# A two-block transformer forward pass: the last product before each run of up products cut in two, and the first norm's factors spread into PSUM by two products

## The chip, the cores and the metric

The kernel runs on one core of a Trainium2 chip, in one launch. The metric is the time of one execution on the device in microseconds (us), lower is better. Before the change the median of three runs is 964.23 us (964.13 to 964.59). Five engines matter here: TensorE (PE) multiplies, its weight loads shown apart as PEld; VectorE (DVE), ScalarE (ACT) and GpSimd (POOL) do everything element by element; SyncE (SP) issues the transfers (DMA).

## The reference, cut to what matters

256 tokens of width 1024 go through two transformer blocks with different mixers, all in float32.

```python
h = rms_norm(x, mix_pre_norm)                       # the first norm: x * rsqrt(mean(x^2) + eps) * factors
mix = hybrid_token_mixer(h, w_in, ...)              # attention, block attention, gated delta rule
x = x + rms_norm(mix, mix_post_norm)
u = causal_depthwise_conv(rms_norm(x, ffn_pre_norm) @ w_up, conv_w) + conv_b
gate, up = split(u)
x = x + rms_norm((gelu(gate) * up) @ w_down, ffn_post_norm)     # 22 blocks up, 11 down
# second model, two layers on the same x
x = x + gmlp_mixer(rmsnorm(x), a_w_in, ..., a_w_out)            # 8 blocks up, 8 down
x = x + square(relu(rmsnorm(x) @ w1_0)) @ w2_0                  # 16 up, 16 down
x = x + mla_mixer(rmsnorm(x), latent_kv(x), ...)
x = x + square(relu(rmsnorm(x) @ w1_1)) @ w2_1                  # 16 up, 16 down
out = rmsnorm(x, final_norm_g)
```

## The kernel before, in words

Tokens lie in two tiles of 128. To keep float32 accuracy every operand of a large product is split into a high and a low part (`split`: ACT copies the high part, DVE subtracts it for the low part), and every product becomes three (`mm3`: high by high, high by low, low by high). In the profile a weight chunk is `raw` when it lands, then `s0h`, `s0l` to `s7h`, `s7l`; normalised tokens are `xTh`, `xTl`; activations between an up and a down product are `aT0h`, `aT0l` and so on.

A large product stands in one of two forms. In `fm` the loaded operand is 128 columns of weights and the streamed one is the 256 tokens (`r_fm<-xTh,s2h 128x256`). In `tm` the loaded operand is one tile of 128 tokens and the weights are streamed: 392 columns in the first projection `w_v`, 256 in the first blocks of a stage, 512 in the down products (`r_acc<-s0h,r_aT0h 128x512`). The names after the arrow are the streamed operand, then the loaded one.

`updown` runs the four feed-forward stages: after a lag of four blocks it alternates `down` (24 products of 512 columns into the four banks `acc0`, `acc1`) with `up` (48 products of 256 columns into `r_fm`; two such ups between two downs in the first feed-forward layer). The last four downs of a stage run together at its end, tile 0 first, and tile 1's part is finished by `last_downs`.

The order of all instructions is made when the kernel is built. Python generators (threads) yield one operation at a time, and `run_threads` always emits the one that an estimate of costs (`Estimate.cost`) says can start first; ranks of 10 and more wait a little. Each engine then works through its own list strictly in that order. So a change of a cost, of a rank or of one operation near the start changes what is chosen for a long way behind it.

Weights come in halves of 128 x 1024 into a ring of four `raw` buffers (`RAW`); `dma_next` issues the next one after a half has been split (`split_piece`). At the start `main` issues, on SP's queue, the two halves of token tile 0, the identity `c_ident`, the 1024 factors of the first norm repeated on 128 partitions (`gb`, 512 KB written), one half of `w_v`, token tile 1, and three more halves. `warm_up` lets PE multiply zeros while nothing else is there, until the estimate says 8 us. `junction` does the first norm of each tile: ACT sums the squares of both halves, DVE and POOL make the root (`rstd`), DVE multiplies x by it and by `gb` (`r_xg`), PE transposes into `r_tp`, ACT and DVE split that into `xTh`, `xTl`.

Of the kernel before, what the change touches and what calls it, by code (L numbers as in the profile page):

```python
# [13 lines left out]
AF = mybir.ActivationFunctionType  # L14
ALU = mybir.AluOpType
AX = mybir.AxisListType

P = 128
D = 1024
EPS = 1e-6  # L20
LAG = 4
TAIL = 4
STAG, STAGF, STAGV = 3, 4, 4
SLOTS, EXTRA, PREF = 4, 1, 10.0
RAW = 4
AHEAD, CLOSE, URGENT = 5, 1, 3
DEFER = 0.3
SLACK = 0.02
WARM = 8.0
BIG = 1e30  # L30
LINE = 128
HALF = LINE // 8
# [1 line left out]
HALVES = (slice(0, 512), slice(512, 1024))  # L34
# [41 lines left out]
class Estimate:  # L76
# [14 lines left out]
    def cost(self, eng, op, aps, args, t):  # L91
        n = max(a.free_size() for a in aps)
        psum = any(a.space == bass.MemoryType.PSUM for a in aps)
        if eng == "PE":
            n = aps[2].free_size() * (4 if aps[1].dtype == F32 else 1) if op == "matmul" else 2 * P
            tick = int(t / self.TICK)
            slow = self.columns.get(tick - 1, 0.0) < 3060.0
            self.columns[tick] = self.columns.get(tick, 0.0) + n * aps[1].partition_size() / P
            return n / 1200.0 if slow else n / 2400.0 + 0.0023
        if eng == "ACT":  # L100
            t = self.TABLES.get(args[2], self.table)
            load, self.table = (1.28 if t != self.table else 0.0), t
            return load + (0.05 if psum else 0.09) + n / 1200.0 + 0.09 * (len(aps) - 2)
        if eng == "DVE":
            if op == "reciprocal":
                return 0.07 + n / 120.0
            fast = not psum and len(aps) == 2 and op in ("tensor_scalar", "tensor_copy")
            return (0.13 if op == "scalar_tensor_tensor" else 0.07) + n / (1920.0 if fast else 960.0)
        return 0.5 if op == "memset" else 0.3 + n / 6.0

    def start(self, use):

# [85 lines left out]
class Kernel:  # L198
# [138 lines left out]

    def can_split(self):
        c = self.chunks.get(self.split_at)
        if c is None or c.pieces == len(c.raw):  # L340
            return False
        return bool(c.pieces or self.free_slots())

# [109 lines left out]
            yield from self.T.transpose(dst[:, b * P:(b + 1) * P], src[:, b * P:(b + 1) * P], self.ident)  # L453


    def mm3(self, o, lh, ll, rh, rl, first, last):
        T = self.T
        yield from T.matmul(o, lh, rh, start=first, stop=False)
        yield from T.matmul(o, lh, rl, start=False, stop=False)
        yield from T.matmul(o, ll, rh, start=False, stop=last)  # L460

    def fm(self, o, w, c0, xT, nk):

# [2 lines left out]
            yield from self.mm3(o, w[0][:, k, c0:c0 + P], w[1][:, k, c0:c0 + P], xT[0][:, k, :], xT[1][:, k, :],  # L466
                     k == 0, k == nk - 1)

    def tm(self, o, w, xT, t, ks, k0=0, c0=0, n=None, first=True, last=True, ev=None):

        n = n or w[0].shape[2]
        ts = slice(t * P, (t + 1) * P)
        for i, k in enumerate(ks):
            yield from self.block_ready(w, k)
            if ev and (k0 + k) % 4 == 0:
                yield self.on((ev, t, (k0 + k) // 4))
            yield from self.mm3(o, xT[0][:, k0 + k, ts], xT[1][:, k0 + k, ts], w[0][:, k, c0:c0 + n], w[1][:, k, c0:c0 + n],
                     first and i == 0, last and i == len(ks) - 1)

    def new_acc(self, t):  # L480
        acc = []
# [1 line left out]
            acc.append((yield from self.bank("acc%d" % t)))  # L483
        return acc

    def down(self, acc, w, aT, t, k0, first, last):
        last = last if isinstance(last, tuple) else (last, last)
        for h in range(2):
            yield from self.tm(acc[h], w, aT, t, (0, 1), k0=k0, c0=h * 512, n=512, first=first, last=last[h])
            if last[h]:  # L490
                self.set(("sum", acc[h].name, 512 * h), acc[h])

# [35 lines left out]
    def junction(self, t, dests, acc=None, post=None):  # L528
# [4 lines left out]
        for g, xT, ev in dests:  # L533
# [15 lines left out]
                self.set((ev, t, h), xT[1])  # L549
            self.set((ev, t), xT[1])  # L550


    def updown(self, names, n, per, pool, block, aT, tail, stagger, gains=(), final=False):

# [26 lines left out]
        for kind, i in updown_plan(n, per):  # L581
# [10 lines left out]
            if acc is None:  # L592
                acc = [[], []]
# [3 lines left out]
            yield self.on((names[0], "block", i))  # L597
            if i < nd - TAIL:
                yield from self.down(acc[0], c.view(2), aT[i], 0, 0, i == 0, False)
                yield from self.down(acc[1], c.view(2), aT[i], 1, 0, i == 0, (False, final and i == nd - TAIL - 1))  # L600
                self.free(c)
                self.rel(aT[i][0])
            else:
                yield from self.down(acc[0], c.view(2), aT[i], 0, 0, i == 0, i == nd - 1)
                last.append((i, c))
# [22 lines left out]
            if cols.stop == D:  # L628
                self.free(c)

    def warm_up(self):

        z = self.tile(self.pers, [P, D], "zero", tag="gb", bufs=2)[:, :P]
        yield from self.G.memset(z, 0.0)
        z = z.bitcast(BF16)
        o = yield from self.bank("acc1")
        while self.est.free["PE"] < WARM:
            yield from self.T.matmul(o[:, :256], z[:, :P], z, start=True, stop=True)
        self.rel(o)
# [28 lines left out]
    def main(self, ctx):  # L668
# [10 lines left out]

        load_x(0)  # L680
        self.ident = self.load(self.consts, "ident")
        g = self.gain("mix_pre_norm")
        self.dma_next()
        load_x(1)
        for _ in range(RAW - 1):
            self.dma_next()
        self.junk_tile = self.tile(self.scr, [P, 512], "junk")
        self.tile(self.scr, [P, 2], "mv", bufs=2)
# [2 lines left out]
        self.one = self.tile(self.consts, [P, 1], "one")  # L691
        yield from self.G.memset(self.one, 1.0)
        self.pad(self.consts, 2 * HALF)
        self.spawn(20, self.warm_up())
        self.hT = self.new_xT()
        for t in range(2):
            self.spawn(0, self.junction(t, [(g, self.hT, "w_in")]))
        with ExitStack() as s:
            yield from self.mixer(self.pool(s, "mix"))
        self.add_slots(self.pool(ctx, "second"), 1)  # L700
# [928 lines left out]
```

## Time and profile before

| | |
|---|---|
| runs | 964.13, 964.23, 964.59 us; median 964.23 |
| the profiled execution | 963.24 us, of which the span is 961.5 |
| PE busy | 939.2 us of the span, 6475 products |
| DVE, ACT, POOL busy | 648.4, 515.0, 24.9 us |
| transfers | 168.22 MB, 175 GB/s over the span |

The span runs from the first to the last instruction. All products and element operations carry one line number, since they are recorded by a helper (L177), so groups are told apart by tile names. PE's products overlap one another (the busy time of one is longer than its distance to the next), so what a stream of products costs is read from the starts, not from the durations.

### The profile page before, as it was taken

The numbers are of one execution on the slowest core, as the hardware profiler recorded it, in microseconds if no ns is written. First come the engines' busy times: TensorE is split into PE (matmuls) and PEld (weight loads), VectorE is DVE, ScalarE is ACT, GpSimd is POOL, SyncE is SP. The second block draws the span as 40 slices with busy tenths as digits, with TensorE's granted clock in tenths as the row PEclk, the third lists the DMA queues.
The fourth block names the chain that finished last, engine by engine and source line by source line (L and its number), as shares of the span: only waits on it lengthen the run. The fifth ranks groups of instructions, "written<-read, shape, count | busy, mean of one in ns | idle before, by whom it ended". The sixth has DMA issues, their size and how long they took to land.

```text
span 961.5 us, 16153 instructions
## 1 busy us (share of the span) xinstructions
PE 939.2 (98%) x6475; PEld 863.1 (90%) x6475; DVE 648.4 (67%) x1027; ACT 515.0 (54%) x853; POOL 24.9 (3%) x38
## 2 busy tenths in 40 slices
PE   7999999999999999999998999999999999999997
PEld 6899878899999989999988999998889899999986
DVE  5687776889687757697557765554678687555533
ACT  5664565767566546535445644444557575444421
POOL 0000000000000001000000000000110000000000
PEclk8999999999999999999999999999999999999999
DMA  7732432746777637727645776564345377566511
GB/s 230 252 111 89 132 110 88 223 132 197 254 227 233 201 113 287 244 88 259 193 133 152 244 226 192 192 194 148 96 149 161 111 231 240 186 202 194 193 47 44
DMA packets 48891, 168.22 MB, mean 175 GB/s; under 512 B 6448, under 2 KB 7088, under 8 KB 48560
## 3 DMA queue, kind: packets, MB, share of 16 engines
q1 hardware_dynamic: 48816, 167.19, 54.5%
q8 instruction: 51, 0.84, 0.4%
q14 instruction: 24, 0.20, 0.1%
HBM read 166.12 MB, written 1.05 MB: 174 GB/s over the span
## 4 chain that ended last, share of the span: by engine, by line
PE 90%; DVE 3%; ACT 2%; DMA 2%; issue 1%; SPq 1%; POOL 0%; POOLq 0%; DVEq 0%; ACTq 0%
PE r_fm L177 47%; PE r_acc L177 38%; PE r_tp L177 5%; DMA x<-x 1%; DMA vm<-inv_freq 1%; ACT junk L177 1%; DVE r_xg L177 1%; DVE cT L177 1%; DMA raw<-w_up 1%; DVE s4l L177 0%; POOL rstd L177 0%; DVE s3l L177 0%; DVE s0l L177 0%; DVE xTl L177 0%; ACT cT L177 0%
## 5 line engine op out<-in xcount | busy, mean ns | idle before, releaser
L177 DVE TENSOR_TENSOR s0l<-raw,s0h 128x1024 fp32r<-128x1024 f32 (+1 forms) x54 | 64.8, 1211 | 19.8 <-ACT s0h L177 19.7
L177 DVE TENSOR_TENSOR s2l<-raw,s2h 128x1024 fp32r<-128x1024 f32 (+1 forms) x54 | 65.1, 1212 | 17.4 <-ACT s2h L177 17.2
L177 DVE TENSOR_TENSOR s3l<-raw,s3h 128x1024 fp32r<-128x1024 f32 (+1 forms) x56 | 66.8, 1201 | 14.9 <-ACT s3h L177 14.7
L177 DVE TENSOR_TENSOR s1l<-raw,s1h 128x1024 fp32r<-128x1024 f32 (+2 forms) x54 | 64.8, 1201 | 15.5 <-ACT s1h L177 15.2
L177 ACT ACTIVATE s0h<-raw 128x1024 fp32r<-128x1024 f32 (+1 forms) x54 | 55.6, 1046 | 26.4 <-PE r_acc L177 17.2
L177 PE MATMUL r_fm<-xTh,s1h 128*128 128x256 f32 x240 | 67.3, 280 | 0.0
L177 PE MATMUL r_fm<-xTl,s1h 128*128 128x256 f32 x240 | 67.3, 280 | 0.0
L177 PE MATMUL r_fm<-xTh,s1l 128*128 128x256 f32 x240 | 67.3, 280 | 0.0
L177 DVE TENSOR_TENSOR s4l<-raw,s4h 128x1024 fp32r<-128x1024 f32 (+1 forms) x46 | 55.2, 1210 | 16.7 <-ACT s4h L177 16.7
L177 ACT ACTIVATE s3h<-raw 128x1024 fp32r<-128x1024 f32 (+1 forms) x56 | 57.5, 1036 | 16.8 <-PE r_acc L177 10.2
L177 ACT ACTIVATE s2h<-raw 128x1024 fp32r<-128x1024 f32 (+1 forms) x54 | 56.0, 1045 | 16.7 <-PE r_acc L177 9.7
L177 DVE TENSOR_TENSOR r_q<-r_r 128x512 f32<-128x512 f32 x32 | 22.1, 692 | 62.1 <-ACT r_r L177 62.0
L177 ACT ACTIVATE s1h<-raw 128x1024 fp32r<-128x1024 f32 (+2 forms) x54 | 55.9, 1037 | 14.4 <-DMA raw<-w_up 5.3
L177 ACT ACTIVATE r_r<-r_fm 128x512 f32<-128x512 f32 x26 | 15.6, 599 | 80.5 <-PE r_fm L177 80.5
L177 ACT ACTIVATE s4h<-raw 128x1024 fp32r<-128x1024 f32 (+1 forms) x46 | 47.4, 1043 | 18.8 <-PE r_acc L177 9.8
L177 PE MATMUL r_fm<-xTh,s3h 128*128 128x256 f32 x200 | 56.3, 281 | 0.4 <-DVE cT L177 0.4
L177 PE MATMUL r_fm<-xTl,s3h 128*128 128x256 f32 x200 | 56.2, 281 | 0.0
L177 PE MATMUL r_fm<-xTh,s3l 128*128 128x256 f32 x200 | 56.1, 281 | 0.0
L177 PE MATMUL r_fm<-xTl,s2h 128*128 128x256 f32 x176 | 49.4, 281 | 0.0
L177 PE MATMUL r_fm<-xTh,s2l 128*128 128x256 f32 x176 | 49.4, 280 | 0.0
L177 PE MATMUL r_fm<-xTh,s2h 128*128 128x256 f32 x176 | 49.3, 280 | 0.0
L177 POOL TENSOR_TENSOR rstd<-rstd,mhalf 128x1 f32<-128x1 f32 (+1 forms) x30 | 23.9, 798 | 931.4 <-DVE rstd L177 914.7
(611 smaller groups left out, 3153.8 us busy)
## 6 DMA issues: line engine op xcount, KB each, us to landing
raw<-w SPq DMA_DIRECT2D x128, 512.0 KB, 4.6
raw<-w_up SPq DMA_DIRECT2D x44, 512.0 KB, 4.8
raw<-w_down SPq DMA_DIRECT2D x22, 512.0 KB, 4.9
raw<-a_v SPq DMA_DIRECT2D x16, 512.0 KB, 5.6
raw<-a_u SPq DMA_DIRECT2D x16, 512.0 KB, 4.5
raw<-a_w_out SPq DMA_DIRECT2D x16, 512.0 KB, 4.7
raw<-w_c SPq DMA_DIRECT2D x12, 512.0 KB, 5.2
raw<-w_out SPq DMA_DIRECT2D x8, 512.0 KB, 3.7
```

The lines of the kernel that those rows point to most:

```text
L177: f(*args, **kw)
```

## The change

The last product of a down block into the second bank of tile 1, 128x512, is issued as two of 128x256 with the same loaded operand (`cut=256`), for all downs but the last four of each stage. The first norm no longer reads its factors from a tile of 128 rows: one row of 4 KB is loaded, and two products with a loaded row of ones (`gain_banks`) spread it into two PSUM banks, behind 16 products of zeros. The square of the second half moves from ACT to DVE. The first weight half may be chosen for splitting only once both normalised halves of tile 0 have been issued, and the next chunks only once tile 0 has been transposed and split. The estimate takes less for a `memset`, and the zeros run on until it says 10 us. Token tile 1 is loaded after two halves of `w_v`, not after one.

```diff
@@ -26,7 +26,7 @@
...
-WARM = 8.0
+COLD, WARM = 16, 10.0
...
@@ -106,7 +106,7 @@
...
-        return 0.5 if op == "memset" else 0.3 + n / 6.0
+        return 0.1 + n / 1280.0 if op == "memset" else 0.3 + n / 6.0
...
@@ -337,7 +337,7 @@
...
     def can_split(self):
         c = self.chunks.get(self.split_at)
-        if c is None or c.pieces == len(c.raw):
+        if c is None or c.pieces == len(c.raw) or ("xg" if self.split_at == 0 else ("w_in", 0)) not in self.ev:
             return False
         return bool(c.pieces or self.free_slots())
...
@@ -453,11 +453,13 @@
...
-    def mm3(self, o, lh, ll, rh, rl, first, last):
+    def mm3(self, o, lh, ll, rh, rl, first, last, cut=None):
         T = self.T
         yield from T.matmul(o, lh, rh, start=first, stop=False)
         yield from T.matmul(o, lh, rl, start=False, stop=False)
-        yield from T.matmul(o, ll, rh, start=False, stop=last)
+        parts = (slice(0, cut), slice(cut, None)) if cut else (slice(None),)
+        for c in parts:
+            yield from T.matmul(o[:, c], ll, rh[:, c], start=False, stop=last and c is parts[-1])
...
         ts = slice(t * P, (t + 1) * P)
...
             yield from self.mm3(o, xT[0][:, k0 + k, ts], xT[1][:, k0 + k, ts], w[0][:, k, c0:c0 + n], w[1][:, k, c0:c0 + n],
-                     first and i == 0, last and i == len(ks) - 1)
+                     first and i == 0, last and i == len(ks) - 1, cut if i == len(ks) - 1 else None)
...
@@ -483,10 +485,11 @@
...
-    def down(self, acc, w, aT, t, k0, first, last):
+    def down(self, acc, w, aT, t, k0, first, last, cut=None):
         last = last if isinstance(last, tuple) else (last, last)
         for h in range(2):
-            yield from self.tm(acc[h], w, aT, t, (0, 1), k0=k0, c0=h * 512, n=512, first=first, last=last[h])
+            yield from self.tm(acc[h], w, aT, t, (0, 1), k0=k0, c0=h * 512, n=512, first=first, last=last[h],
+                               cut=cut if h else None)
             if last[h]:
                 self.set(("sum", acc[h].name, 512 * h), acc[h])
...
@@ -548,6 +551,45 @@
...
+    def gain_banks(self, row):
+
+        banks = []
+        for h in HALVES:
+            o = yield from self.bank("acc0", row)
+            yield from self.T.matmul(o, self.one[:1, :].to_broadcast([1, P]), row[:, h], start=True, stop=True)
+            banks.append(o)
+        self.first_gain = banks
+        self.set("first gain", *banks)
+
+    def first_norm(self, t):
+
+        S, V, x = self.S, self.V, self.x[t]
+        ss = self.sums()
+        if t:
+            yield self.on(("w_in", 0, 0))
+        yield from S.activation(self.junk(512), x[:, HALVES[0]], AF.Square, accum_out=ss[:, 0:1])
+        xg = []
+        for h in range(2):
+            xg.append((yield from self.take(self.scr, [P, 512], "xg")))
+        yield from V.scalar_tensor_tensor(xg[1], x[:, HALVES[1]], 1.0, x[:, HALVES[1]], op0=ALU.mult, op1=ALU.mult,
+                                          accum_out=ss[:, 1:2])
+        r = yield from self.rstd(ss, 1, D, 2)
+        yield self.on("first gain")
+        for h in range(2):
+            yield from V.scalar_tensor_tensor(xg[h], x[:, HALVES[h]], r, self.first_gain[h], op0=ALU.mult, op1=ALU.mult)
+        self.set("xg")
+        if t:
+            self.rel(*self.first_gain)
+        for h in range(2):
+            tp = yield from self.bank("tp", xg[h])
+            yield from self.transposes(tp, xg[h], 4)
+            self.rel(xg[h])
+            sl = (slice(None), slice(4 * h, 4 * h + 4), slice(t * P, (t + 1) * P))
+            yield from self.split(self.hT[0][sl], self.hT[1][sl], tp.rearrange("p (k c) -> p k c", k=4))
+            self.rel(tp)
+            self.set(("w_in", t, h), self.hT[1])
+        self.set(("w_in", t), self.hT[1])
...
@@ -597,7 +639,8 @@
...
             if i < nd - TAIL:
                 yield from self.down(acc[0], c.view(2), aT[i], 0, 0, i == 0, False)
-                yield from self.down(acc[1], c.view(2), aT[i], 1, 0, i == 0, (False, final and i == nd - TAIL - 1))
+                yield from self.down(acc[1], c.view(2), aT[i], 1, 0, i == 0, (False, final and i == nd - TAIL - 1),
+                                     cut=256)
                 self.free(c)
...
@@ -628,12 +671,15 @@
...
-    def warm_up(self):
+    def warm_up(self, row):
 
         z = self.tile(self.pers, [P, D], "zero", tag="gb", bufs=2)[:, :P]
         yield from self.G.memset(z, 0.0)
         z = z.bitcast(BF16)
         o = yield from self.bank("acc1")
+        for _ in range(COLD):
+            yield from self.T.matmul(o[:, :256], z[:, :P], z, start=True, stop=True)
+        self.spawn(0, self.gain_banks(row))
         while self.est.free["PE"] < WARM:
             yield from self.T.matmul(o[:, :256], z[:, :P], z, start=True, stop=True)
         self.rel(o)
@@ -679,10 +725,13 @@
 
         load_x(0)
         self.ident = self.load(self.consts, "ident")
-        g = self.gain("mix_pre_norm")
-        self.dma_next()
+        row = self.tile(self.pers, [P, D], "row", tag="gb", bufs=2)[:1, :]
+        self.nc.sync.dma_start(row, ap["mix_pre_norm"][None, :])
+        self.est.dma(row, 4 * D)
+        for _ in range(2):
+            self.dma_next()
         load_x(1)
-        for _ in range(RAW - 1):
+        for _ in range(RAW - 2):
             self.dma_next()
...
-        self.spawn(20, self.warm_up())
+        self.spawn(20, self.warm_up(row))
         self.hT = self.new_xT()
         for t in range(2):
-            self.spawn(0, self.junction(t, [(g, self.hT, "w_in")]))
+            self.spawn(0, self.first_norm(t))
```

PE, at the start of the program (rows 37 to 42 of the changed kernel; `zero` is the tile of zeros, `row` the row of factors, `one` a column of ones). The zeros ahead and behind are the same pair of rows again.

```order
L177 LDWEIGHTS zero
L177 MATMUL r_acc_111<-zero 128x256
L177 MATMUL r_acc_134<-row,one 128x512
L177 MATMUL r_acc_136<-row,one 128x512
L177 LDWEIGHTS zero
```

There are 19 products of zeros ahead of the two new ones; behind them stand 11, then four transposes of `r_xg`, 5 zeros, four transposes, 10 zeros and the first product of `w_v`. Before, 26 zeros, four transposes, 3 zeros and four transposes stood ahead of it.

DVE, at the start of the program, before (`x_74` and `x_75` are the two token tiles).

```order
L177 TENSOR_TENSOR rstd<-ss 128x1
L177 TENSOR_SCALAR rstd<-rstd 128x1
L177 SCALAR_TENSOR_TENSOR r_xg<-x_74,rstd,gb 128x512 x2
L177 TENSOR_TENSOR s0l<-raw,s0h 128x784
L177 TENSOR_TENSOR xTl<-r_tp,xTh 128x4x128
L177 TENSOR_TENSOR rstd<-ss 128x1
L177 TENSOR_SCALAR rstd<-rstd 128x1
L177 TENSOR_TENSOR xTl<-r_tp,xTh 128x4x128
L177 SCALAR_TENSOR_TENSOR r_xg<-x_75,rstd,gb 128x512 x2
L177 TENSOR_TENSOR s0l<-raw,s0h 128x784
```

The same place of DVE's list in the changed kernel.

```order
L177 SCALAR_TENSOR_TENSOR r_xg,ss<-x_74 128x512
L177 TENSOR_TENSOR rstd<-ss 128x1
L177 TENSOR_SCALAR rstd<-rstd 128x1
L177 SCALAR_TENSOR_TENSOR r_xg<-x_74,rstd,r_acc_134 128x512
L177 SCALAR_TENSOR_TENSOR r_xg<-x_74,rstd,r_acc_136 128x512
L177 TENSOR_TENSOR s0l<-raw,s0h 128x784
L177 TENSOR_TENSOR xTl<-r_tp,xTh 128x4x128
L177 TENSOR_TENSOR s0l<-raw,s0h 128x784
L177 TENSOR_TENSOR xTl<-r_tp,xTh 128x4x128
L177 SCALAR_TENSOR_TENSOR r_xg,ss<-x_75 128x512
L177 TENSOR_TENSOR s1l<-raw,s1h 128x784
```

Both halves of the first weight chunk now stand ahead of everything of token tile 1, whose norm has moved behind them.

PE, at the product that waits for the gates of the delta rule (`gates`, made by ACT and DVE from the columns of `w_v`), with the difference to before.

```order
 L177 MATMUL r_fm<-xTh,s3l 128x256
 L177 MATMUL r_fm<-xTh,s3h 128x256
+L177 MATMUL r_fm<-xTl,s3h 128x256
+L177 MATMUL r_fm<-xTh,s3l 128x256
+L177 MATMUL r_fm<-xTh,s3h 128x256
+L177 MATMUL r_fm<-xTl,s3h 128x256
+L177 MATMUL r_fm<-xTh,s3l 128x256
+L177 MATMUL r_fm<-xTh,s3h 128x256
 L177 MATMUL r_tp<-gates,c_mix_consts 128x8
 L177 MATMUL r_tp<-gates,one 128x8
```

Six products of the projection that runs there have moved ahead of it. Behind this place PE's list differs for some 517 products of the mixer (different ones chosen first, the same ones in all); from the end of its attention on, it is the same as before but for the cuts.

PE, at the end of the first down block of the first feed-forward layer, in the changed kernel (`r_acc_2684` is the second bank of tile 1).

```order
L177 MATMUL r_acc_2684<-s0h,aT0l 128x512
L177 MATMUL r_acc_2684<-s0h,r_aT0h 128x512
L177 MATMUL r_acc_2684<-s0l,r_aT0h 128x512
L177 MATMUL r_acc_2684<-s0h,aT0l 128x256 x2
L177 MATMUL r_fm<-xTh,s1h 128x256
L177 MATMUL r_fm<-xTl,s1h 128x256
```

Before, the row with x2 was one product `128x512`. There are 35 such places; behind 31 of them stands a run of up products (six runs of 96, three of 48, twice eleven of 48), behind the other four the last downs of the stage.

## Rows read from the trace of the kernel before

**Rows 1.** The page, part 1: engine, busy us, share, instructions.

```profile
PE 939.2 (98%) x6475; PEld 863.1 (90%) x6475; DVE 648.4 (67%) x1027; ACT 515.0 (54%) x853; POOL 24.9 (3%) x38
```

**Rows 2.** Busy time by stretch (window, length, each engine's busy us, granted clock, DMA).

```profile
12.00:20.00 8.00, 6.96 (x32) 5.53 (x32) 7.39 (x12) 5.56 (x9) 0.56 (x1) 0.81 0.53 158
...
42.00:152.00 110.00, 108.60 (x848) 97.30 (x847) 89.23 (x211) 66.97 (x168) 5.58 (x6) 1.00 0.37 118
...
515.00:690.00 175.00, 175.00 (x1128) 159.91 (x1128) 104.18 (x131) 85.93 (x116) 0.55 (x1) 1.00 0.58 182
```

**Rows 3.** The chain that ended last, up and down blocks (start us, us, what).

```profile
232.58 5.46 PE r_acc L177 x24
238.03 11.31 PE r_fm L177 x96
...
544.08 5.65 PE r_fm L177 x48
```

**Rows 4.** The same view, runs of 256 columns elsewhere.

```profile
200.95 30.16 PE r_fm L177 x266
...
379.88 24.15 PE r_fm L177 x205
...
407.91 10.20 PE r_fm L177 x90
...
525.14 1.77 PE r_fm L177 x15
...
527.26 1.94 PE r_fm L177 x17
```

**Rows 5.** Timeline of PE (start us, us, engine, line, op, out<-streamed,loaded).

```profile
198.49 0.28 PE L177 MATMUL r_fm<-s4h,xTl 128*128 128x256 f32 x1
...
198.94 0.28 PE L177 MATMUL r_fm<-xTh,s0h 128*128 128x256 f32 x1
...
199.42 0.28 PE L177 MATMUL r_fm<-xTl,s0h 128*128 128x256 f32 x1
```

**Rows 6.** Timeline of the start, all engines (in brackets idle time before, and its releaser).

```profile
1.06 4.78 PE L177 MATMUL r_acc<-zero 128*128 128x256 bf16 x26 [1.06 <-POOL zero L177]
...
2.11 0.43 SPq L294 DMA_DIRECT2D gb<-mix_pre_norm  x1
...
5.68 0.55 POOL L177 TENSOR_TENSOR rstd<-rstd,mhalf 128x1 f32<-128x1 f32 x1 [4.68 <-DVE rstd L177]
8.77 1.41 DVE L177 SCALAR_TENSOR_TENSOR r_xg<-x,rstd,gb 128x512 f32<-128x512 f32 x2 [3.24 <-DMA gb<-mix_pre_norm]
...
9.84 0.86 ACT L177 ACTIVATE s0h<-raw 128x784 fp32r<-128x784 f32 x1 [4.69 <-DMA raw<-w_v]
...
11.84 0.68 PE L177 MATMUL r_fm<-s0h,xTh 128*128 128x392 f32 x1
...
21.11 1.23 DVE L177 TENSOR_TENSOR s2l<-raw,s2h 128x1024 fp32r<-128x1024 f32 x1 [0.80 <-ACT s2h L177]
```

**Rows 7.** DMA issues of the first 30 us (KB each, median us to landing).

```profile
c_ident<-ident SPq DMA_DIRECT2D x1, 64.0 KB, 4.3
```

**Rows 8.** All products of zeros (ns min/median/max, first and last start).

```profile
L177 PE MATMUL r_acc<-zero x29: 272/421/421, 1.1 to 10.9; 128*128 128x256 bf16 x29
```

**Rows 9.** Busy time in two stretches of 1 us, as in rows 2.

```profile
7.00:8.00 1.00, 0.00 (x0) 0.00 (x0) 0.00 (x0) 0.00 (x0) 0.00 (x0) 1.00 1.00 387
8.00:9.00 1.00, 0.00 (x0) 0.00 (x0) 0.23 (x1) 0.00 (x0) 0.00 (x0) 0.57 1.06 408
```

**Rows 10.** Timeline around the first projections and the gates.

```profile
24.50 0.28 PE L177 MATMUL r_fm<-xTh,s2h 128*128 128x256 f32 x1
...
31.29 1.06 ACT L177 ACTIVATE s1h<-raw 128x1024 fp32r<-128x1024 f32 x1 [1.76 <-DMA raw<-w_c]
...
36.67 0.36 PE L177 MATMUL r_tp<-gates,c_mix_consts 128*128 128x8 f32 x2 [2.35 <-issue]
...
40.52 1.72 PE L177 MATMUL r_acc<-c_mix_consts,gates 128*128 128x128 f32 x14
```

More of the change, by code (lines that the diff above doesn't have):

```diff
@@ L467, in fm, with tm @@
                      k == 0, k == nk - 1)
-    def tm(self, o, w, xT, t, ks, k0=0, c0=0, n=None, first=True, last=True, ev=None):
+    def tm(self, o, w, xT, t, ks, k0=0, c0=0, n=None, first=True, last=True, ev=None, cut=None):
         n = n or w[0].shape[2]
```

## The prediction

> **What bounds the kernel now.** I read the page's first part, the busy times by stretch, the chain of waits through the feed-forward stages, and the timeline of the first 40 us. PE is busy for 939.2 of 961.5 us [rows 1]; through the stages of up and down blocks it never pauses (175.00 of 175 us) while DVE has 104 and ACT 86 us of work there [rows 2]. So two things can move the end: what one product costs in those stages, and what PE waits for at the start.
>
> The reader is to see in the chain of waits what a product costs. Down: 24 in 5.46 us, 0.2275 each. Up: 96 in 11.31, 0.1178 each; 48 in 5.65, the same [rows 3]. But there are runs of the same shape at another distance: 266 in 30.16 is 0.1134, 90 in 10.20 is 0.1133, 205 in 24.15 is 0.1178 [rows 4]. So 256 columns have two levels, 0.1134 and 0.1178, and a run keeps its level for hundreds of products. All the runs of up products that follow a down block lie at the higher one.
>
> Where does the level change? In the pieces 379.88 and 407.91 PE does not pause between the two: the stage goes over from the token-major form to the feature-major one (the streamed and the loaded operand change places) and falls from 0.1178 to 0.1133. Pieces 525.14 (15 in 1.77, 0.118) and 527.26 (17 in 1.94, 0.114) lie on either side of the same exchange [rows 4]. At 198.94 the exchange finds a run at the lower level, four in 0.45 us, and leaves it at the higher, four in 0.48 [rows 5]. So in these three cases an exchange between products of 256 columns turns the level over. After a down block the exchange comes too, but with it the change from 512 to 256, and the run is at the higher level.
>
> At the start PE waits for the first norm. Its factor is there at 5.68 + 0.55 = 6.2 us, but DVE begins the normalised halves at 8.77, having waited for the factors that are repeated on 128 rows; the first product of `w_v` starts at 11.84 [rows 6]. From then on DVE is full (7.39 of 8 us) [rows 2] until it has the second remainder of the next weight chunk at 21.11 + 1.23 = 22.3 [rows 6], and PE starts that projection at 24.50 [rows 10].
>
> **The cut.** It divides 35 products. Two of 256 columns at the higher level are 0.2356 against 0.2275: 35 x 0.008 = 0.3 us lost. Behind 31 of them stands a run of ups, 6 x 96 + 3 x 48 + 22 x 48 = 1776 products. Now the last thing ahead of the exchange is two products of 256 columns in the token-major form, which is the situation of [rows 4], no longer 512 columns. If the exchange turns the level over as it did there, the runs fall to 0.1134: 1776 x 0.0044 = 7.8 us won, all of it on the path, since PE is the only full engine there. The first products behind an exchange may still stand at the higher spacing; for three of them at each of 31 entries I take off 0.4. Sum: -7.8 + 0.3 + 0.4 = -7.1. The ends are +0.3 (no run changes) and -7.8 (every one, the cut itself free). I take the end with the turn, because the three exchanges between equal sizes are the nearest rows to the new order; the runs after 512 columns are the nearest to the old one.
>
> The Trainium skill (TensorE: Matmul & The Clock Gate, Back-to-back issue gap) gives one gap for one size, columns by the full clock plus about 2.5 ns, and nothing on what stood ahead. By that rule the cut would cost 35 x 2.5 ns = 0.09 us as an estimate, and win nothing, which is rival 1 below. The trace has two levels for one size [rows 4], so it does not agree.
>
> **The start.** The row of 4 KB takes the broadcast's place in SP's queue, right behind the identity, which lands 4.3 us after its issue at about 1.64, so at 5.9 [rows 6, 7]. I take 5.9 for the row too. On PE it is queued behind 19 products of zeros. Zeros come at two speeds (421 and 272 ns) [rows 8]: 256 columns are 0.213 us at 1.2 GHz and 0.107 at 2.4, and 26 in 4.78 us fit 17 slow and 9 fast ones. So 19 end near 1.06 + 17 x 0.213 + 2 x 0.11 = 4.9, and PE waits about 1 us. A float32 product of 128 columns shows as two records: 14 records in 1.72 us are seven products, 0.21 to 0.25 each [rows 10], so one of 512 columns is about 0.86 at full clock. The factors are in PSUM at 6.8 and 7.6, DVE's first normalised half starts at about 7.0 instead of 8.77. Behind them on PE stand 26 more zeros (2.8 us) and eight transposes (0.11 each, 0.9): the first product of `w_v` cannot start before 7.6 + 3.7 = 11.3, 0.5 earlier than before. The zeros hide nothing here; they stand ahead of the transposes.
>
> What counts is DVE's list, which is the bound until 22.3. It began at 8.77 and took 13.6 us; the changed list is the same plus one square of 128x512 (the other falls into the wait), priced by the normalising row, 1.41 / 2 = 0.7 [rows 6]. A factor read from PSUM instead of a tile of 128 rows has no row; I take the same duration, between none and 0.1 more for each of four. Starting at 7.0 it would end at 21.3; the waits for weights in the old list shrink, since the broadcast's 512 KB are gone from the queue and the first weight half no longer lands only at 9.84. Lower end 7.0 + 13.6 - 0.8 (the wait at 21.11) = 19.8, upper end 22.3. I take 20.8: -1.5 us at 24.50.
>
> Next is the product that waits for the gates: PE idles 2.35 us ahead of it, at 36.67, and the chain goes back to a weight half that landed at 31.29 [rows 10]. That half's buffer is freed by DVE's list, so it comes 1.5 earlier as well. In PE's new order six more products (6 x 0.113 = 0.7) stand ahead of it and fill part of the wait. Start and gates together: -2.2, ends 0 and -3.7 (the whole 2.35 filled with -1.4 ahead of it).
>
> **The mixer's order** is another one for 517 products. PE is idle for 1.4 of the 110 us there [rows 2], so at best 1.4 is won; as much may be lost. I take 0.
>
> **Sum.** -7.1 - 2.2 = -9.3. The profiled execution took 963.24, 0.99 below the median 964.23, so it would become 953.9, and the median 954.9.
>
> **Rivals.** (1) *The level stays.* A run after down products is at 0.1178 wherever one follows [rows 3], and two products between may be too few to change what 512 columns have set. Against it stand [rows 4, 5]. Then -2.2 + 0.3: 962.3.
> (2) *The start is given back.* Rival 1, and what is ahead at 24.50 is lost in the mixer's new order, where PE's strict list meets other waits: +0.3, at most a stall or two of about 1 us: 964.5. For it: the order is made by an estimate that left 2.35 us of waiting at the gates. Against: only 1.4 us of idle time there so far.
> (3) *The row comes late; slower.* PE's list is strict, so everything waits behind the two factor products. Before, PE stopped at 5.8, and the granted clock was 1.00 in the window from 7 us and 0.57 in that from 8 [rows 9]: it fell after 2 to 3 us of rest. If the row lands as late as the broadcast did, near 8.6, PE has rested 3.7 us and works at half clock: two factors 3.4 us, 26 zeros 5.5, transposes 1.7, so `w_v` starts at 19.2 instead of 11.84, and its 48 products of 392 columns (0.163 each at 2.4 GHz, 7.8 us) end at 27.0, 2.5 later than 24.50. With the runs at the old level: 964.2 + 0.3 + 2.5 = 967.0. It decides from a landing of about 7.5 on. Against it: 4 KB instead of 512.
>
> **Chances.** Forecast 0.65, by itself 952.7 (all ends good) to 957.5 (a part of the runs turns). Rival 1 0.18, rival 2 0.10, rival 3 0.07. About 0.2% (1.93 us: below 962.3 and above 966.2) is what a measurement tells from no change. Faster: 0.65 and half of rival 1, 0.74. Same: the other half and rival 2, 0.19. Slower: 0.07. The range reaches over rival 1 into rival 2, 952.0 to 964.5, and leaves out the others with half of rival 2, and a little below.
>
> **What would show it.** In the chain of waits, pieces of 48 ups of 5.45 us instead of 5.65 and of 96 of 10.9 instead of 11.31, beside down pieces of 5.46; the first product of `w_v` near 11.3, the projection at 24.50 near 23.0, the wait at the gates under 1.7. Wrong: up pieces still at 5.65 and the time at 962 (rival 1), that and an idle time in the mixer of 3 us (rival 2), or a granted clock of 0.5 while the zeros run behind the factors (rival 3).

## The result, and the profile after

The five executions of the changed kernel took 956.09, 956.88, 960.05, 961.25 and 3311.51 us, a median of 960.05 beside 964.13 of the kernel before (963.34 to 964.59). The last one was disturbed and does not count in the ratio: the other four have a median of 958.47, ratio 0.9942, 95% interval 0.9921 to 0.9962. In a second series (`after_again`, below) the changed kernel took 956.60 (954.39 to 961.16) beside 965.62: 0.9909 (0.9890 to 0.9928). It is faster in both; 954.9 was predicted. Its times spread over 5 us in the first series and 7 in the second, which the prediction did not expect; the experiments explain a part of that.

The profiled execution took 956.88 (before 963.24). Part 1 of its page answers [rows 1], the busy times by stretch answer [rows 2]; the columns are those named there.

```profile
PE 935.2 (98%) x6531; PEld 859.5 (90%) x6531; DVE 648.8 (68%) x1031; ACT 515.1 (54%) x849; POOL 26.4 (3%) x38
```

```profile
12.00:20.00 8.00, 6.53 (x38) 5.87 (x38) 7.52 (x14) 4.75 (x6) 1.23 (x1) 1.00 0.76 251
42.00:152.00 110.00, 107.64 (x832) 95.96 (x831) 86.86 (x201) 67.52 (x166) 7.39 (x6) 1.00 0.33 106
515.00:690.00 175.00, 175.00 (x1151) 159.81 (x1150) 104.44 (x126) 88.88 (x123) 2.56 (x3) 1.00 0.58 184
```

In the last window PE still never pauses. Its 1151 products beside 1128 are no measure of the win, since 24 of them are halves of divided products and the window lies some 4 us further on in the program. PE's busy time fell by 4.0 us although 56 instructions came to it. The chain of waits of the changed kernel says where, and answers [rows 3]:

```profile
230.34 5.46 PE r_acc L177 x25
235.80 10.90 PE r_fm L177 x96
...
440.34 5.46 PE r_fm L177 x48
```

96 ups take 10.90 instead of 11.31, 48 take 5.46 instead of 5.65, and the down piece with its one product more still 5.46. All 31 runs behind a division show this. The start, in the timeline of all engines, answers [rows 6, 10]:

```profile
1.06 3.83 PE L177 MATMUL r_acc<-zero 128*128 128x256 bf16 x19 [1.06 <-POOL zero L177]
...
2.11 0.33 SPq L729 DMA_DIRECT2D row<-mix_pre_norm  x1
...
4.82 1.98 PE L177 MATMUL r_acc<-row,one 1*128 1x512 f32 x4
...
5.80 0.55 POOL L177 TENSOR_TENSOR rstd<-rstd,mhalf 128x1 f32<-128x1 f32 x1 [4.79 <-DVE rstd L177]
6.38 1.41 DVE L177 SCALAR_TENSOR_TENSOR r_xg<-x,rstd,r_acc 128x512 f32<-128x512 f32 x2 [0.74 <-POOL rstd L177]
...
10.37 0.42 PE L177 MATMUL r_fm<-s0h,xTh 128*128 128x392 f32 x1
```

The row is there by 4.82, and PE goes from the zeros to the factors almost without a stop (two starts 0.20 us apart), where before it stood idle for 3.73 us ahead of the first transposes. DVE now waits for POOL's factor (0.74), no longer for the load (3.24). The normalising of two halves reads PSUM at the old price, 1.41. Where the granted clock stood at 0.57 in the microsecond from 8 [rows 9], it is 1.00:

```profile
7.00:8.00 1.00, 1.00 (x12) 0.91 (x10) 0.79 (x2) 0.60 (x1) 0.00 (x0) 1.00 0.98 368
8.00:9.00 1.00, 1.00 (x11) 0.94 (x10) 0.71 (x1) 0.68 (x2) 0.00 (x0) 1.00 1.06 412
```

From the first starts of the same products in the timelines of PE, the program falls into eight stretches. Three of the experiments stand beside the two (us):

| stretch, up to | before | after | cut_only | start_only | early_again |
|---|---|---|---|---|---|
| first w_qk product | 24.50 | 21.97 | 24.92 | 21.95 | 22.47 |
| exchange at 199 (mixer, out, w_up) | 174.44 | 174.78 | 175.36 | 174.27 | 174.84 |
| token-major a_v at 361 | 162.12 | 159.77 | 161.03 | 162.06 | 161.04 |
| token-major w1 at 503 | 142.36 | 141.87 | 141.88 | 142.36 | 141.88 |
| exchange at 527 | 23.68 | 25.09 | 24.43 | 25.57 | 18.91 |
| token-major w1 at 775 | 247.74 | 246.03 | 246.03 | 247.87 | 245.97 |
| exchange at 794 | 18.82 | 19.64 | 19.12 | 20.28 | 18.94 |
| last product | 160.79 | 158.95 | 159.34 | 160.79 | 158.95 |

Between before and after: the start -2.53, the mixer +0.34, the four stretches with divisions -2.35 - 0.49 - 1.71 - 1.84 = -6.39, and two junctions, which nobody had touched, +1.41 and +0.82. Sum -6.35.

### The profile page after: what moved, and what is told of

Read it like the earlier page. It is cut to its first block, busy times and chain, and to the rows that moved or that the text cites. A ratio compares the mean times of both kernels' runs of the same rounds, so it can differ in the third digit from the quotient of the medians.

```text
span 955.1 us, 16271 instructions
## 1 busy us (share of the span) xinstructions
PE 935.2 (98%) x6531; PEld 859.5 (90%) x6531; DVE 648.8 (68%) x1031; ACT 515.1 (54%) x849; POOL 26.4 (3%) x38
## 4 chain that ended last, share of the span: by engine, by line
PE 88%; DVE 4%; DMA 2%; ACT 2%; issue 1%; POOL 1%; SPq 1%; POOLq 0%; DVEq 0%; ACTq 0%
PE r_fm L177 46%; PE r_acc L177 37%; PE r_tp L177 5%; DMA vm<-inv_freq 1%; POOL rstd L177 1%; ACT junk L177 1%; DVE r_xg L177 1%; DMA raw<-w_v 1%; DMA raw<-w 1%; DVE s1l L177 0%; DVE xTl L177 0%; DMA raw<-w_up 0%; DVE s4l L177 0%; DVE s0l L177 0%; DVE s3l L177 0%
```

## The experiments

**Each half of the change alone, the change again, and the division in another place.** The kernel before with the division only (`cut_only`), the changed kernel with `cut=None` (`start_only`), the changed kernel unedited (`after_again`), and the kernel before with the division in the first half of the block:

```diff
-                               cut=cut if h else None)
+                               cut=None if h else cut)
```

> The kernel before with the 35 divided products alone; start and mixer as before. Theory (two products of 256 columns ahead of the exchange turn the runs of up products to the lower level, 0.1134 to 0.1138 instead of 0.1178): 31 runs, 6 x 0.41 + 25 x 0.19 = 7.2 us less, 957.0, with pieces of 96 in 10.9 and of 48 in 5.46. Rival A (the level is set by something that the new start shifts, a phase that lasts through the program): the runs stay at 11.31 and 5.65, 964.4. Rival B (each entry falls to one level or the other at random): the trace shows some runs at 5.65 and some at 5.46, and the time spreads over several us.

> The changed kernel without the divided products: the row, the factors in PSUM, the new start and the mixer's new order. Theory (the start is worth 3.5 us at the gates, of which the mixer gives back 1.3, and nothing else changes): 964.1 - 2.2 = 961.9, runs of ups at 11.31 and 5.65. Rival A (the changed start also turns the runs): 955 to 957. Rival B (the 2.0 us that the changed kernel lost again at the junctions near 503 and 783 us come from the start, not from the cut): 963.9.

> The changed kernel once more, unedited, for a second trace and five more times: it had 956.1 to 961.3 where the kernel before had 963.3 to 964.6. Theory (the entries to a level are chancy, and what varies is how many runs and token-major stages get the lower one): the times again lie between 956 and 961.5, and a stage-by-stage comparison of the two traces differs in the spacing of products (0.1134 against 0.1178), not in idle time. Rival (what varies is a wait, at the start or for a weight): the spacings are the same and PE's idle time differs by the difference of the spans.

> The kernel before with the same 35 divisions one half earlier: the last product of acc[1]'s first half is divided, so that six undivided products of 512 columns stand between it and the exchange. Theory (it is what stands right ahead of the exchange that sets the level): runs stay at 11.31 and 5.65, 964.1 + 35 x 0 to 0.008 = 964.1 to 964.4. Rival (a division anywhere in the block, one product more, is enough): 957.0 with runs at 10.9 and 5.46.

Measured, as ratios to the kernel before on the same chip: cut_only 0.9936 (0.9924 to 0.9948), start_only 0.9996 (0.9981 to 1.0011), after_again 0.9909 (0.9890 to 0.9928), cut_early 1.0001 (0.9990 to 1.0011). The same run of 48 ups in the chain of cut_only, of start_only and of cut_early:

```profile
445.14 5.46 PE r_fm L177 x48
```

```profile
442.10 5.65 PE r_fm L177 x48
```

```profile
445.18 5.65 PE r_fm L177 x48
```

So the division, and it alone, brings the lower level behind the downs, and only where it stands last: with six undivided products of 512 columns between it and the ups they stay at the higher one. The start has no part in it. In start_only the first w_qk product comes at 21.95 as in the changed kernel, but the end hardly moves: the table has +1.89 and +1.46 at the junctions. Its theory (961.9) missed; the profiled execution took 963.96, the time of its rival B.

after_again has the changed kernel's stretches within 0.7 us, with the idle time at 503 to 527 again (4.1 us). Its span is 1.3 us shorter, and both of its ways have a part in that. Near 783 PE idles 0.09 us instead of 0.69, which is the rival, a wait. The other 0.6 us are the theory, a level: of two executions of one program one has the same run of the mixer at 0.118 and the other at 0.114. In the changed kernel's first trace and then in after_again's:

```profile
38.79 14.38 PE r_fm L177 x122
```

```profile
38.71 13.86 PE r_fm L177 x122
```

**What the junction near 503 waits for.** PE's transposes wait there for DVE's normalised half (3.83 us in the changed kernel). DVE in that kernel:

```profile
501.82 0.16 DVE L177 CAST vm<-c_pos 128x2 f32<-128x2 int32 x1
506.76 0.24 DVE L177 TENSOR_SCALAR vm<-vm 128x32 f32<-128x32 f32 x1 [4.78 <-DMA vm<-inv_freq]
506.91 1.41 DVE L177 SCALAR_TENSOR_TENSOR r_xg<-x,rstd,gb 128x512 f32<-128x512 f32 x2
```

The norm is queued behind an instruction for the angles that waits for 16 KB of frequencies, issued at 499.06 behind five other constants and three halves of weights. `early_freq` loads them one stage earlier, into a tile of the size of a pad:

```diff
-        self.pad(self.consts, 2 * HALF)
+        self.fr = self.tile(self.consts, [P, 32], "fr")
...
         lnb = self.bcast(self.tile(pool, [P, 2048], "lnb"), "ln_b")
+        self.bcast(self.fr, "inv_freq")
...
-        fr = self.bcast(scratch[:, 128:160], "inv_freq")
+        fr = self.fr
```

> The changed kernel with one small load moved: the 32 frequencies of the angles come in the stage before, into a tile of their own, instead of being issued at 499 us behind five other constants. In all traces so far DVE waits 3.4 to 5.0 us for that load near 506, the second tile's normalising stands behind the wait, PE idles 2.4 to 4.1 us for it and its granted clock falls to 0.86 to 0.93 over the stage. Theory (that landing is what moves by chance and makes the stage 22.0 to 25.6 us long): the stage becomes 20 to 21 us, the time falls by 3.5 to 952 to 953 where the changed kernel has 956.6, and the spread of the times shrinks. Rival (the norm is late anyway, for its factor or its rows of gains): DVE waits for another releaser, PE still idles 2 us or more, the time falls by less than 1.

Measured: 952.61, ratio 0.9880 (0.9859 to 0.9900). The stretch is 18.84 instead of 25.09. DVE there, and PE with the granted clock, in early_freq and then in the changed kernel:

```profile
505.31 1.41 DVE L177 SCALAR_TENSOR_TENSOR r_xg<-x,rstd,gb 128x512 f32<-128x512 f32 x2 [0.21 <-POOL rstd L177]
```

```profile
501.00:520.00 19.00, 19.00 (x163) 18.87 (x162) 16.93 (x40) 11.74 (x21) 0.62 (x1) 1.00 0.66 192
```

```profile
498.40:523.50 25.10, 21.27 (x162) 21.09 (x161) 16.87 (x39) 11.89 (x21) 0.55 (x1) 0.86 0.55 147
```

The theory held, and its size for the stretch was too small: the wait was 3.8 us, the stretch lost 6.2. The rest goes with the granted clock: in the changed kernel it is 0.50 from 506.1 to 512.9, and in that time PE does four transposes in 1.09 us, where early_freq needs 0.60, and starts products of 256 columns 0.213 us apart instead of 0.118. The expectation has the clock falling in all traces so far; in cut_early it did not (last section). By ratios the time fell from 0.9909 to 0.9880, 2.8 us, a little less than the 3.5 forecast. In the eight traces with the late load the stretch varies from 21.97 to 25.57, which is a part of the spread of their times. The spread did shrink, but not to nothing: 4.1 us here, 3.2 in a second series (`early_again`, below).

What sets the landing is not chance alone, so far as the traces show. From its issue to its landing the load takes 6.20, 6.55 and 6.98 us in the three traces with the old start, and 7.28 to 7.84 in all five with the new one; in the chain of before and of the changed kernel:

```profile
504.08 6.98 DMA vm<-inv_freq
```

```profile
499.06 7.61 DMA vm<-inv_freq
```

That speaks for rival B of start_only: the new start loses a part of its win again at this load. By which way a start can reach a load 480 us later no run shows.

**Other sizes of the pieces.** The changed kernel with 384 and 128 columns (`cut=384`), and with 128 and 384 (`cut=128`).

> The changed kernel with the 35 products divided into 384 and 128 columns instead of 256 and 256. Theory A (it is enough that the last product ahead of the exchange is shorter than 512, so that the run is entered with the pipe in another phase): runs of ups at 10.9 and 5.46, time as the changed kernel's, within 1 us. Theory B (the rows spoke only of exchanges between equal products of 256): the runs go back to 11.31 and 5.65, 6.5 us more than the changed kernel; a product of 128 columns may also cost more than its columns, up to 0.05 us each, 1.7 in all.

> The same with 128 and then 384 columns, so that a product of 384 stands right ahead of the exchange. Theory A (any shorter product last): 10.9 and 5.46 again. Theory B (equal products of 256 only): 11.31 and 5.65, 6.5 us more. Theory C (what counts is that the last product is no longer than the ones that follow): back to the higher level here, the lower one with 128 last.

Measured: 0.9958 (0.9938 to 0.9979) and 0.9966 (0.9950 to 0.9982). The run of 48 near 440 in the one and in the other:

```profile
441.13 5.51 PE r_fm L177 x48
```

```profile
444.05 5.47 PE r_fm L177 x48
```

Theory A holds for the level: both are at the lower one, so two equal products are not needed, and a last product of 384 is enough. For the time it missed. It forecast the changed kernel's within 1 us, and the ratios are 0.005 to 0.006 above its 0.9909, some 5 us. An unequal division costs more: a block of 48 ups and its downs takes 10.97 and 10.98 instead of 10.92, 1.9 us for 35. Between the profiled executions of the first of the two and of the changed kernel, 958.82 and 956.88, that is the whole difference; where the rest of the 5 us comes from is not shown.

**Ahead of the token-major stages.** Where downs are followed by products of the same form, the last of 512 is divided too:

```diff
-                                   first=fresh and m == 0, last=m == len(items) - 1)
+                                   first=fresh and m == 0, last=m == len(items) - 1,
+                                   cut=256 if m == len(items) - 1 and cols == HALVES[1] else None)
```

First on the changed kernel (`cut_tail`), then with the early load (`freq_tail`), since the profiled execution of the first took 5335.49 us and none of its rows is used.

> The changed kernel with five more products divided: the last one of 512 columns ahead of each token-major stage (at 169, 356, 498, 769 us and ahead of the latents). There the next products have the same form, so no operand changes places. Theory (the exchange between products of 256 columns turns the level; two pieces alone do not): the token-major runs that follow stay at 0.1178, no change of the time beyond 0.04 us. Rival (any two products of 256 columns behind those of 512 bring the lower spacing, and it stays): the four runs that follow directly, 61 + 78 + 46 + 47 products, at 0.1134, 1.0 us less, and up to 3 us if the runs behind their transposes keep it too.

> The changed kernel with the early load of the frequencies and the five more divided products ahead of the token-major stages (their first trial left no trace that can be read). Theory (without an exchange the level stays): the runs at about 170, 359, 501 and 766 us at 0.1178, time as the kernel without them, ratio 0.988. Rival (a shorter product last is enough, exchange or not, as the unequal cuts suggest for the runs of ups): those runs at 0.1134, 1.0 to 1.5 us less, ratio 0.9865 or below.

Measured: 0.9911 (0.9884 to 0.9938) and 0.9882 (0.9862 to 0.9902), against 0.9909 and 0.9880 or 0.9864 without it: no gain. The chain of freq_tail has the 78 products at a_v at 9.18 / 78 = 0.118:

```profile
360.01 9.18 PE r_fm L177 x78
```

The three other runs are at 0.1177 or 0.1178. The theory's forecast held here; for its reason see the last experiment.

**The start's worth without the late load.** `cut_freq` is the kernel before with the division and the early load; `early_again` is early_freq unedited, on the same chip as cut_freq.

> The kernel before with the divided products and the early load of the frequencies, but with the old start. Beside the kernel with both and the new start (952.6 where the kernel before had 963.9, ratio 0.9880) it gives the start's worth at the end of the program with the chancy wait near 506 us out of the way. Theory (the start is worth the 2.3 to 2.9 us that the traces show at 199 us, and start_only showed only 0.5 of it because its wait for the frequencies was 0.7 longer and its junctions fell badly): 2.3 to 2.9 us slower than the kernel with both, ratio 0.990 to 0.991. Rival (what the start wins is lost again in the later stages in any case): ratio 0.988, the same.

> The changed kernel with the early load once more, unedited, on the same chip as the two others. Theory: ratio 0.988 again, the stage between 501 and 520 us within 0.5 of the 18.84 it had, no wait of DVE for the frequencies. Rival (the 18.84 was a lucky landing): 20 us or more.

Measured: cut_freq 954.07, 0.9889 (0.9871 to 0.9908); early_again 952.09, 0.9864 (0.9843 to 0.9885). The start is worth 2.0 us of the medians, and 2.3 between the last products of the two traces (945.30 and 943.00); the intervals overlap, so the medians alone would not tell the two apart. That is at the lower end of the theory's 2.3 to 2.9, and the ratio lies between the theory's and the rival's: most of what the start wins reaches the end once the load is out of the way. early_again's stretch at 503 is 18.91 again, cut_freq's 18.74, freq_tail's 18.72. early_freq is the version that beats both kernels: twice 0.986 to 0.988 where the changed kernel had 0.991 to 0.994.

**A division inside a run.** On early_freq, one product in the middle of a token-major run and the last of the up block behind each staggered stage become two of 128 columns:

```diff
-                o = yield from self.up(c.view(8), xT)
+                o = yield from self.up(c.view(8), xT, cut=128 if stagger and i == stagger else None)
...
-            yield from self.tm(o, w.view(8), hT, t, range(8), ev="a_v")
+            yield from self.tm(o, w.view(8), hT, t, range(8), ev="a_v", cut=128 if (c, t) == (STAGV, 1) else None)
```

> The changed kernel with the early load of the frequencies, and four products of 256 columns in the middle of long runs divided into two of 128: one in the token-major run at 369 us (at 0.1178 in every trace, 156 products stand ahead of the division and 144 behind it), and the last up product of the block behind each staggered stage (in the feature-major runs at 200, 522 and 786 us; that at 200 has been at the lower level in six traces and at the higher in six, the two others nearly always at the lower). Theory (what turns the level is the exchange behind a shorter product): the token-major run stays at 0.1178 behind its division, the feature-major runs keep whatever level they have, and the time is that of the kernel without these divisions, 952 (ratio 0.986 to 0.988). Rival (any shorter product shifts the pipe, and the lower level is the one it falls to): 0.1134 behind the division in all four, 0.6 us less at 369 and up to 1.1 us less at 200, ratio 0.985 to 0.987. A third way (a shorter product shifts it to a level by chance): some of the runs that are at the lower level go up behind it.

Measured: 0.9871 (0.9849 to 0.9893), no difference in time. But the rows decide. PE around the division at 206 (feature-major), four products on each side:

```profile
205.84 0.28 PE L177 MATMUL r_fm<-xTh,s0h 128*128 128x256 f32 x1
...
206.32 0.28 PE L177 MATMUL r_fm<-xTl,s0h 128*128 128x256 f32 x1
206.43 0.33 PE L177 MATMUL r_fm<-xTh,s0l 128*128 128x128 f32 x2
...
208.04 0.28 PE L177 MATMUL r_fm<-xTh,s1h 128*128 128x256 f32 x1
...
208.50 0.28 PE L177 MATMUL r_fm<-xTl,s1h 128*128 128x256 f32 x1
```

Four spacings in 0.48 us ahead of it, four in 0.46 behind; over the 38 ahead the spacing is 0.1178, over the rest of the run 0.1135. The first products behind the division still start 0.116 to 0.122 apart, up to 207.25, and from there on 0.113; the first ones behind a divided down do the same. The chain has this run of 280 (281 with the division) at 32.04, between the 31.77 of traces that enter it low and the 32.98 of those that enter high. The two other feature-major runs were low and stayed low. The token-major run at 389 stays at 0.1178 behind its division:

```profile
389.60 0.28 PE L177 MATMUL r_fm<-s4l,xTh 128*128 128x256 f32 x1
...
390.55 0.28 PE L177 MATMUL r_fm<-s4h,xTh 128*128 128x256 f32 x1
```

Eight spacings in 0.95. Theory and rival both fall. In the feature-major form the spacing dropped behind a shorter product with no exchange near; that is one run in one trace, the only one of the three that stood high. In the token-major form it did not drop in five places. The third way, a level by chance, is not ruled out by one run, though in none of the twelve other traces does the level change inside this one.

## Why the prediction was right, and where it was not

The time of 960.05 lies in the stated range, 952.0 to 964.5, but 5.1 us above the forecast; in the second series the kernel moved by -9.0 of the -9.3 forecast.

**The cut: right in sign and size, wrong in its reason.** -7.1 was forecast, -6.39 came in the trace, and cut_only gives 0.9936 of 964, -6.2 us. The win of the runs was right: 6 x 0.41 + 25 x 0.19 = 7.2 against 7.8 less 0.4 for the entries. The mis-sized term is the division itself: a block of 48 ups and its downs takes 11.09 us in start_only and 10.92 here, so 0.17 stays of 0.19, and a division costs 0.02, not 0.008; 0.6 in all instead of 0.3.

The step that failed is "an exchange between products of 256 columns turns the level over". The changed kernel itself has an exchange of equal products at 523.48, amid this piece of its chain, and goes on at 4.24 / 36 = 0.1178 on both sides, where before the same place fell [rows 4]:

```profile
521.52 4.24 PE r_fm L177 x36
```

The thirteen traces have 52 such exchanges, near 199, 404, 523 and 790. The nine that are entered at the lower level leave at the higher one. Of the 43 entered at the higher one 32 fall and eleven stay, this one among them. So what the prediction read from three cases holds in 41 of 52: it is a tendency, not a rule.

Which level the run of 280 near 199 takes is chance so far as the runs show: 31.75 to 31.78 us in six traces, 32.98 in six others, with either start among both. And in cut_inside it dropped behind a division with no exchange near. What the runs bear out is narrower, and for the place behind a down block alone: a run of ups that follows 512 columns directly is at 0.1178 (31 of 31 in each of the three traces that have such runs); one that follows a divided product, whose last piece has 256, 384 or 128 columns, is at 0.1135 to 0.1149 with its first products (31 of 31 in each of the ten others), and at 0.1133 to 0.1134 behind them. Why stays open. The forecast drew the right conclusion because the cut puts exactly such a product there; that its rule, which needs equal products on both sides of the exchange, pointed the same way was luck in part, since unequal pieces do as well.

**The start and the mixer: the sum was right, with two errors that cancel.** Forecast: -1.5 at the projection, -2.2 with the gates, 0 in the mixer. The projection came 2.5 earlier: the row landed before 4.8, not at 5.9, and the first w_v product started at 10.37, not 11.3. With the gates it was -3.5, from 36.67 to 33.14. The wait at the gates fell from 2.35 to 0.68, as forecast ("under 1.7"):

```profile
33.14 0.36 PE L177 MATMUL r_tp<-gates,c_mix_consts 128*128 128x8 f32 x2 [0.68 <-issue]
```

By the exchange at 199 -2.2 was left, the forecast sum: the mixer's new order gave 1.3 back, where 0 was taken. That the two errors cancel is luck. In the nine traces with the new start PE waits 1.56 us for DVE in the mixer, near 53 in the changed kernel, which no trace with the old start has; the run of 122 at the higher level (above) costs this execution another 0.6, and other places win some of it back.

```profile
54.72 0.36 PE L177 MATMUL r_fm<-xTh,s3h 128*128 128x256 f32 x1 [1.56 <-DVE cT L177]
```

The price of a factor in PSUM was taken at nothing extra, rightly. A factor product took 0.96 from start to next start, not 0.86; the row's early landing paid for that.

**What was not in the sum: the junctions.** +1.41 and +0.82 in the profiled execution, 2.2 of the 3.0 us by which it missed the 953.9 forecast for it. The prediction looked for late waits at the start and in the mixer, and read the stages behind as never pausing; but before, PE idled 3.2 us ahead of 512.21 for the same load. That wait was in the trace, DVE's releaser there was a DMA, and its length differs from trace to trace. At the second junction PE idles 0.69 us at 786.9, before not at all: ACT's copy that it waits for stands behind a `split`, which had waited 1.13 us for a weight half.

**Rivals.** Rival 1 (the level stays) is refuted by cut_only; the slowest counted execution, 961.25, came near its time, and has no trace. Rival 2 (the mixer gives the start back): the mixer gave back 1.3 of 3.5, no more. Rival 3 (the row late, the clock low) did not happen through the row, which was early in all traces. Its price did appear once, in cut_inside: there the factors take 3.78 us instead of 1.98 and the first w_v product starts at 14.95.

```profile
5.22 3.78 PE L177 MATMUL r_acc<-row,one 1*128 1x512 f32 x4
...
14.95 0.42 PE L177 MATMUL r_fm<-s0h,xTh 128*128 128x392 f32 x1
```

## What to carry to other kernels

When one shape shows two spacings in a trace, look at what stands right ahead of each run, and test a one-product change there: 0.0044 us on 1776 products outweighed what was won at the waits of the start. Before pricing a change, list every wait of the critical engine whose releaser is a DMA, also far from the edit: a 16 KB load behind five others, with an in-order engine waiting for it, made its stretch 22.0 to 25.6 us long and hid what the edit won. Compare kernels by stretches as well as by times, since stretches that differ by 1 to 6 us buried the start's 2.3.

## What the runs showed of the hardware that was not expected

- Products of 256 columns have two stable spacings, 0.1133 to 0.1134 and 0.1177 to 0.1179 us behind their first products, at a granted clock of 1.00 in both. Two executions of one program can differ in it. A divided product ahead came with the lower one for feature-major runs alone; token-major runs kept 0.1178 behind five divisions, though short ones reach 0.1133 at times (25 products near 182 us). Why the form matters stays open.
- A rest of 3.8 us cost PE 2.4 us more than the rest itself (a stretch of 25.09 against 18.84), while in cut_early a rest of 2.4 left the granted clock at 1.00:

```profile
503.80:525.80 22.00, 19.17 (x162) 18.77 (x161) 16.66 (x39) 11.86 (x21) 0.55 (x1) 1.00 0.58 166
```

- At the start the new kernel draws too: the first w_v product came at 10.31 to 11.98 in eight traces and at 14.95 in one. In that one the 11 zeros behind the factors take 2.53 us and start 0.21 apart, the spacing of 256 columns at 1.2 GHz; in the changed kernel they take 1.38 and start 0.11 apart, the spacing at 2.4. The profile's clock reads 1.00 in both, but it does so from 1 to 4 us of the changed kernel too, where the zeros start 0.21 apart, so it tells nothing of the first microseconds. In early_freq, with 11.98, it is 0.50 from 7.2 to 10.6. What sets the moment was not tried.

```profile
8.93 2.05 PEld L177 LDWEIGHTS <-zero 128*128 128x128 bf16 x11 [1.50 <-issue]
8.94 2.53 PE L177 MATMUL r_acc<-zero 128*128 128x256 bf16 x11
```

- A product of one row and 512 float32 columns shows as two records that start 0.43 us apart; two such products take 1.91 us to the start of the next one.
